# Decays computed beside the triangular inverse in a bidirectional RWKV-7 / GLA trunk, with root, share and block-deal settings changed

## The chip, the cores and the metric

One core of one Trainium2 chip runs the whole program. The metric is the device time of one execution in microseconds (us); the kernel before has a median of 1413.8 us over three runs (1413.56 to 1420.72).

The engines are named as in the profile: PE (TensorE matmuls; PEld its weight loads), DVE (VectorE), ACT (ScalarE), POOL (GpSimd), SP (SyncE, which issues most DMAs). A name such as L806 is a line of the kernel before.

## The reference, cut to what matters

Two layers of a trunk run on 640 tokens (128 of a prompt, 512 of a sample), width 1024. Layer 0 has a short gated convolution and a bidirectional RWKV-7 mixer with 16 heads of 64; layer 1 is chunked gated linear attention. The change touches layer 0 alone, and in it these quantities of the RWKV-7 mixer, for two directions:

```
w_raw = w0 + tanh(h @ w1) @ w2
decay = exp(-exp(-softplus(-w_raw) - 0.5))
iclr  = sigmoid(a0 + (h @ a1) @ a2)
kk    = k * k_k;  kk = kk / max(sqrt(sum(kk * kk)), 1e-12)
k_mod = k * (1 + (iclr - 1) * k_a)
s     = s * w_t - (s @ kk_t) (kk_t * a_t) + v_t k_t        (token by token)
gn    = (o - mean(o)) * rsqrt(var(o) + 64e-5)
bonus = sum(r * (k_mod of both directions) * r_k) * v
```

`iclr` is called the rate below. The kernel does the recurrence in chunks of 64 tokens: a chunk needs the running products of the decays, a masked 64 by 64 matrix G, and the inverse of a unit triangular part of it.

## The kernel before, in words

**Order.** Matrix instructions on PE run in the order in which the program writes them. Instructions of the other engines are placed by a scheduler at compile time: each engine takes the ready instruction of the best priority, so work can be pulled ahead of where it is written, until a tile that it needs is still held by an earlier user. Each tile name (tag) has a fixed number of buffers.

**Periods.** The 16 heads are taken as 8 pairs. After a prologue (head pair 0) come periods 0 to 7; period hp runs the state chain of pair hp, in 8 steps (`chain_step`, L957) of 6 gaps each, and prepares pair n = hp + 1 in these 48 gaps. Each gap also gets a share of the dense matmuls: blocks of 48 matmuls of 320 columns (`dense`), which project the input for v, k, r, z of the pairs and for the convolution tiles. `Period` (from L1151) deals the blocks' cost (a planner's 134 ns a matmul) to the gaps in proportion to `base` plus the planner's costs of the small work due in the gap; `share` multiplies the weights of some gaps (the prologue's gaps 5 to 9 by `psh`). `CN` and `NC0` say how many of the 32 convolution blocks go to which place. In a paired gap (all periods but the prologue) small work stands before the dense matmuls of an even gap and behind those of an odd gap.

**Small work of a period** (`period`, L1275; lists of gaps in `PR`):
- `expand_all` (L809), eight units at the gaps of `ex`: the first two are `expand` (L747) for direction 0, chunks 0 to 4 and 5 to 9; the other six are `pairs` (L792), PE's matmuls for G of 4, 4 and 2 chunks in each direction, their masked evictions on DVE (L806), and, with the first two, `expand` for direction 1. `expand` makes Pq and iP (exp of the decays' running sums, ACT L757 and L758), the operands `ar` and `bk` on DVE (L765 to L790). Pq and iP have one buffer each, and Pq shares it with `X_i`, the state at the start of the chain (L923).
- `inv_a` (L871) at the gap `inv`: G's triangular 32 by 32 blocks go to DRAM and back as 80 lanes (`Ai`), are inverted there by 30 pairs of dependent DVE instructions (L880, L882), and go back by DRAM into G. `Ai` is a tile of the tag `lw`, which also holds the decays.
- `inv_b` (L894) at `ib`: DVE transposes (L902) and PE's `pT` matmuls complete the inverse.
- `bonus` (L854) at `bo`: adds the two directions' modified rates (L857), multiplies by r (L858), then the sums on PE.
- `p_lr` (L448) for the pair after, at `lr`, when `bonus` is done: for the rates (tags `ta0`, `ta1`) and then the decays (`lw`), four times two PE matmuls (`plr_ta`, `plr_lw`) and an ACT tanh (L478); for the decays also two ACT scalings (L482) and four DVE scans (L487). Its weights come by two DMAs (L453), an ACT rounding (L455) and a POOL difference (L461).
- `p_kk` and `p_kb` (L709, L735): norms of kk; `fin_s`, `fin_b`, `fin_t` (L1054 to L1110): group norm and gate of the pair before; `chain_init`, `vrows`.

`p_kk` and `fin_s` call `rsqrt` (L207), a bit trick and three Newton rounds: 11 DVE instructions on 10 columns. Other norms of the kernel use POOL's power instruction (L286, L1622).

**Around the periods.** The prologue has 32 unpaired gaps. Period 6 loads six stored convolution tiles back (`load_conv`, L1197), two of them into `lw`; period 7 starts the output projection and uses `ta0`, `ta1` and `lw` for parts of a later modulation (`gemv`, L1257). Layer 1 follows and is not touched.

Of the kernel before, what the change touches and what calls it, by code (L numbers as in the profile page):

```python
# [127 lines left out]
def tile_trunk(ctx, tc, A, O):  # L128
# [319 lines left out]
    def p_lr(hp):  # L448
# [16 lines left out]
        lw, ta = [], []
        for (lst, i, boff, tg) in ((ta, 1, 16, "ta"), (lw, 0, 0, "lw")):
            if not i:
                low(0, raw0)
                lwt = el.tile([P, 2, TOK], F32, tag="lw", name=f"lw{hp}")
            for d in range(2):  # L470
                o = et(f"{tg}{d}", f"{tg}{hp}_{d}") if i else lwt[:, d]
                b = der[:, boff + d * 8 + hp:boff + d * 8 + hp + 1]
                for s in range(2):
                    ps = pm(f"plr{hp}_{d}_{tg}_{s}")
                    t = slice(s * HT, (s + 1) * HT)
                    mm(ps[:, 0:HT], w2h[i][:, d], hlr[i, d][:, t], start=True, stop=False)
                    mm(ps[:, 0:HT], w2l[i][:, d], hlr[i, d][:, t], start=False, stop=True)
                    evict(lambda: S.activation(o[:, t], ps[:, 0:HT], AF.Tanh, scale=0.5, bias=b))  # L478
                    yield 270
                lst.append(o)  # L480
# [1428 lines left out]
```

## Time and profile before

| what | value |
|---|---|
| median of three runs | 1413.8 us |
| the profiled execution | 1424.3 us, of which the span is 1422.5 us |
| mean granted TensorE clock | 0.949 of full speed |
| PE busy | 1307.4 us (92%) |
| DVE busy | 960.6 us (68%) |
| ACT, POOL busy | 739.0 us (52%), 461.8 us (32%) |

The profiled execution is one run, 10.5 us longer than the median. PE's busy time counts matmuls at whatever clock was granted; the granted clock has two levels, 1.2 and 2.4 GHz, which the profile shows as 0.5 and 1.0. A row of the timeline gives the start and the length in us, the engine, the line, the operation, the tiles written and read, the shapes, the count of merged instructions, and in brackets the idle time before it with what ended it.

The prologue's dense part runs from about 55 us to 189 us of the span, periods 0 to 7 from there to about 1020 us.

### The profile page before, as it was taken

The page shows a single profiled execution, that of the slowest core. Times are in us where ns is not written, and L with a number is a line of the kernel's source. Part 1 is how long each engine was busy: PE and PEld are TensorE (multiplying, and loading weights), DVE is VectorE, ACT ScalarE, POOL GpSimd, SP SyncE. Part 2 cuts the span into 40 slices and gives each one's busy share as a digit, 9 for nine tenths or more (in the row PEclk, how much of TensorE's full clock was granted, in tenths as well). Part 3 has the DMA queues.
Part 4 walks back from the last instruction along what each step waited for, and adds up shares of the span by engine and source line. Part 5 has one row for each costly group of instructions (what it writes and reads, how often), then busy time and mean ns, then how long its engine had stood idle before and what let it go on. Part 6 is the DMA issues. An engine that isn't in the chain of part 4 may idle for free.

```text
span 1422.5 us, 32431 instructions
## 1 busy us (share of the span) xinstructions
PE 1307.4 (92%) x12279; PEld 1193.4 (84%) x12279; DVE 960.6 (68%) x2218; ACT 739.0 (52%) x2054; POOL 461.8 (32%) x596
## 2 busy tenths in 40 slices
PE   8889899998998988989989989789989999999997
PEld 3779888987887977978978968779889889999997
DVE  5375646977776885786686778675966596646454
ACT  3553264575565565555746655544445764434341
POOL 1433332222222222222322213334466343343232
PEclk9988998999999999989989999788999999999998
DMA  9112222212212212212212232455644322322143
GB/s 355 59 57 79 66 66 57 63 61 67 64 59 61 68 44 70 66 46 71 68 44 60 69 80 65 122 176 162 185 126 137 99 70 79 98 86 85 53 130 105
DMA packets 139629, 127.15 MB, mean 89 GB/s; under 512 B 54096, under 2 KB 121936, under 8 KB 139472
## 3 DMA queue, kind: packets, MB, share of 16 engines
q1 hardware_dynamic: 136912, 118.38, 28.0%
q0 software_dynamic: 2016, 6.16, 1.1%
q8 instruction: 97, 1.59, 0.5%
q14 instruction: 60, 0.49, 0.1%
q10 hardware_dynamic: 544, 0.52, 0.1%
HBM read 108.37 MB, written 16.65 MB: 88 GB/s over the span
## 4 chain that ended last, share of the span: by engine, by line
PE 45%; DVE 26%; ACT 4%; DMA 4%; issue 4%; POOL 1%; SPq 0%; POOLq 0%; DVEq 0%; ACTq 0%
PE pd_zg L135 4%; PE pd_oo L135 4%; PE pd_zw L135 3%; PE pd_qk L135 3%; PE pd_k L135 3%; DVE Ai L882 3%; PE pu L135 3%; PE pd_zc L135 3%; DVE Ai L880 2%; PE pd_eoc L135 2%; PE pd_gc L135 2%; PE pa L135 2%; DVE gacc L247 2%; PE pd_vg L135 2%; DVE bk L790 2%
## 5 line engine op out<-in xcount | busy, mean ns | idle before, releaser
L880 DVE TENSOR_TENSOR Ai<-Ai 80x30 f32<-80x30 f32 (+14 forms) x240 | 95.1, 396 | 36.9 <-DMA Ai<-Ad 30.0
L882 DVE TENSOR_TENSOR Ai<-Ai 80x30 f32<-80x30 f32 (+14 forms) x240 | 96.8, 403 | 6.8
L135 PE MATMUL pG<-ar,bk 64*128 64x128 f32 x640 | 69.5, 325 | 30.8 <-DVE bk L790 18.4
L135 PEld LDWEIGHTS pG<-ar,bk 64*128 64x128 f32 x640 | 54.0, 215 | 45.3 <-DVE bk L790 18.4
L806 DVE TENSOR_TENSOR G<-pG,con 128x512 f32<-128x512 f32 (+1 forms) x96 | 53.2, 595 | 23.5 <-PE pG L135 23.1
L247 DVE SCALAR_TENSOR_TENSOR gacc<-gw,cf,gacc 128x512 f32<-128x512 f32 x70 | 60.2, 891 | 10.1 <-DMA gw<-in_ada_dram 9.8
L1022 ACT ACTIVATE VU<-pa 64x192 f32<-64x192 f32 (+1 forms) x128 | 38.3, 299 | 55.0 <-PE pa L135 53.8
L333 POOL TENSOR_TENSOR lo_eoc<-wr_eoc,hi_eoc 128x256 fp32r<-128x256 f32 x48 | 44.9, 946 | 45.7 <-ACT hi_eoc L330 35.1
L1037 DVE SCALAR_TENSOR_TENSOR X<-pu,PC,XP 128x64 f32<-128x64 f32 x144 | 33.1, 274 | 27.4 <-PE pu L135 24.8
L333 POOL TENSOR_TENSOR lo_gc<-wr_gc,hi_gc 128x256 fp32r<-128x256 f32 x32 | 27.8, 876 | 70.9 <-ACT hi_gc L330 70.1
L333 POOL TENSOR_TENSOR lo_gb<-wr_gb,hi_gb 128x256 fp32r<-128x256 f32 x32 | 25.4, 800 | 73.5 <-ACT hi_gb L330 44.4
L135 PE MATMUL pd_gc<-hi,hi_gc 128*128 128x320 f32 x128 | 43.4, 339 | 4.5 <-ACT cy L446 2.1
L333 POOL TENSOR_TENSOR lo_zw<-wr_zw,hi_zw 128x256 fp32r<-128x256 f32 x32 | 27.2, 861 | 62.7 <-ACT hi_zw L330 56.3
L135 PE MATMUL pd_eoc<-hi,lo_eoc 128*128 128x320 f32 x128 | 44.0, 343 | 3.2 <-POOL lo_eoc L333 3.2
L991 ACT ACTIVATE XP<-X,PC 128x64 f32<-128x64 f32 x120 | 35.8, 342 | 21.1 <-DVE X L1037 20.8
L135 PE MATMUL pd_zc<-hi,hi_zc 128*128 128x320 f32 x128 | 42.7, 334 | 4.3 <-DVE cv L683 2.5
L333 POOL TENSOR_TENSOR lo_r<-wr_r,hi_r 128x256 fp32r<-128x256 f32 x32 | 25.0, 787 | 65.5 <-ACT hi_r L330 51.5
L333 POOL TENSOR_TENSOR lo_zc<-wr_zc,hi_zc 128x256 fp32r<-128x256 f32 x32 | 24.8, 781 | 65.3 <-ACT hi_zc L330 60.6
L333 POOL TENSOR_TENSOR lo_u<-wr_u,hi_u 128x256 fp32r<-128x256 f32 x32 | 26.8, 840 | 59.2 <-ACT hi_u L330 56.8
L135 PE MATMUL pd_k<-hi,hi_k 128*128 128x320 f32 x112 | 37.3, 333 | 9.4 <-ACT k L446 3.8
L135 PE MATMUL pd_eoc<-hi,hi_eoc 128*128 128x320 f32 x128 | 44.9, 351 | 0.9 <-ACT hi_eoc L330 0.9
L333 POOL TENSOR_TENSOR lo_k<-wr_k,hi_k 128x256 fp32r<-128x256 f32 x28 | 23.5, 841 | 65.1 <-ACT hi_k L330 63.8
(482 smaller groups left out, 5075.9 us busy)
## 6 DMA issues: line engine op xcount, KB each, us to landing
gw<-in_ada_dram SPq DMA_DIRECT2D x64, 256.0 KB, 3.2
gw<-in_ada_dram SPq DMA_DIRECT2D x16, 512.0 KB, 7.9
wr_eoc<-in_eo_dram SPq DMA_DIRECT2D x48, 128.0 KB, 2.7
wr_qk<-in_ow_dram SPq DMA_DIRECT2D x33, 128.0 KB, 2.3
wr_r<-in_ew_dram SPq DMA_DIRECT2D x32, 128.0 KB, 2.4
wr_v<-in_ew_dram SPq DMA_DIRECT2D x32, 128.0 KB, 2.5
wr_u<-in_ew_dram SPq DMA_DIRECT2D x32, 128.0 KB, 2.3
wr_gc<-in_ew_dram SPq DMA_DIRECT2D x32, 128.0 KB, 2.3
```

The lines of the kernel that those rows point to most:

```text
L135: tc.keep_in_program_order(T.matmul(*a, **kw))
L247: V.scalar_tensor_tensor(acc[j], w, c, acc[j], op0=ALU.mult, op1=ALU.add)
L333: le.tensor_tensor(lo, w, hi.bitcast(F32), op=ALU.subtract)
L790: E(2).tensor_tensor(bk[HS[h], :, h], ta3[HS[h]], iP3[HS[h]], op=ALU.mult)
L806: V.tensor_tensor(g, x, mk, op=ALU.mult)
L880: V.tensor_tensor(tt, Ai[:, 0:i, i:i + 1].to_broadcast([80, i, n]), Ai[:, i:i + 1, i + 1:].to_broadcast([80, i, n]), op=ALU.mult)
L882: V.tensor_tensor(Ai[:, 0:i, i + 1:], Ai[:, 0:i, i + 1:], tt, op=ALU.add)
L991: S.activation(XP[:, l], X[:, l], AF.Copy, scale=PC[:, s, l:l + 1])
L1022: S.activation(VU[HB[h], h, 0:nl], pr[HB[h], 0:nl], AF.Copy, scale=-1.0)
L1037: V.scalar_tensor_tensor(Xn[:, l], po[:, 0, l], PC[:, s, l:l + 1], XP[:, l], op0=ALU.mult, op1=ALU.add)
```

## The change

- `p_lr` is split in two parts with generators of their own: the decays (part 0) at gaps 17 to 21 (`lrw`) as soon as the pair's G is made, and the rates (part 1) at gaps 43 to 47 as soon as the inverse is written. Each part loads its own weights. The rates of both directions are now one tile of the tag `ta`.
- `Ai` takes the tag `ta` in place of `lw`. The two DVE instructions at the head of `bonus` become `bonus_a`, due just before `inv_a`.
- `ex` goes from gaps 0, 1, 5, 7, 9, 11, 12, 13 to 0, 1, 4, 5, 6, 8, 9, 10; `inv` from 14 to 11; `fb`, `ft` from 14 and 17 to 20, to 12 and 13 to 16. Period 0 keeps its `ex0` and `inv0`; its rates' and decays' order is exchanged.
- `rsqrt` becomes one POOL power instruction, for its 16 calls.
- `psh` goes from 0.1 to 1.0, `pib` (the prologue's `inv_b`) from gaps 28 to 31 to gaps 30 to 31. One convolution block more in the prologue (`NC0` 8), one less in period 1; period 6 takes its convolution blocks ahead of z.
- `load_conv` puts tiles 4 and 5 into `ta`; `gemv` uses `ta` as one tile.

The diff, cut:

```
-PR = {'NC0': 7,
- 'CN': [[2, 1, 1], [2, 1, 1], [1, 1, 1], [1, 1, 1], [1, 1, 1], [1, 1, 1], [2, 1, 1]],
+PR = {'NC0': 8,
+ 'CN': [[2, 1, 1], [1, 1, 1], [1, 1, 1], [1, 1, 1], [1, 1, 1], [1, 1, 1], [2, 2, 2]],
+ 'lrw': [17, 21],
- 'pib': [28, 31],
+ 'pib': [30, 31],
- 'psh': 0.1,
+ 'psh': 1.0,
- 'ex': [0, 1, 5, 7, 9, 11, 12, 13],
- 'inv': 14,
+ 'ex': [0, 1, 4, 5, 6, 8, 9, 10],
+ 'inv': 11,
- 'lr': [39, 47],
+ 'lr': [43, 47],
- 'fb': 14,
- 'ft': [17, 20],
+ 'fb': 12,
+ 'ft': [13, 16],
...
     def rsqrt(x, n):
-        y, t = (cst.tile([P, 20], F32, tag=g, name=f"{g}{next(ids)}")[:, 0:n] for g in ("rsy", "rst"))
...
+        G.tensor_tensor(x, x, mhalf[:, 0:n], op=ALU.pow)
...
-    def p_lr(hp):
+    def p_lr(hp, part):
...
-        low(1, load(1))
-        raw0 = load(0)
+        low(part, load(part))
         yield 0
...
+        boff, tg = ((0, "lw"), (16, "ta"))[part]
+        x = el.tile([P, 2, TOK], F32, tag=tg, name=f"{tg}{hp}")
...
+        for d in range(2 if not part else 0):
+            S.activation(x[:, d], x[:, d], AF.Identity, scale=-0.5 * CW, bias=mcw)
...
+    def bonus_a(hp):
+        q = st[hp]
+        ta, r = q["ta"], q["r"]
+        E(7).tensor_tensor(ta[0], ta[0], ta[1], op=ALU.add)
+        E(8).tensor_tensor(r, ta[0], r, op=ALU.mult)
+        yield 0
...
-        At = el.tile([80, 2 * TOK], F32, tag="lw", name=f"Ai{hp}")
+        At = el.tile([80, 2 * TOK], F32, tag="ta", name=f"Ai{hp}")
...
-                misc += [Work(PRE, p_lr(n + 1), 9, *PR["lr" if hp else "lr0"], 270, (n, "b")), ...
+                misc += [Work(PRE, p_lr(n + 1, 0), 5, *PR["lrw"], 270, (n, "g")), Work(PRE, p_lr(n + 1, 1), 5, *PR["lr"], 270, (n, "i")), ...
```

The last argument of a `Work` is what it needs: "g" is G made, "i" the inverse written, "b" the bonus done. The settings of period 6 (`ex6`, `inv6`, `fb6`, `ft6`) change as `ex`, `inv`, `fb`, `ft` do.

## Rows read from the trace of the kernel before

**Rows 1.** The page: TensorE's granted clock in 40 slices of the span

```profile
PEclk9988998999999999989989999788999999999998
```

**Rows 2.** Windows: stretch, us, busy us (instructions) by engine, PE's clock, DMA

```profile
93.40:113.90 20.50, 14.93 (x74) 12.19 (x75) 16.32 (x32) 6.23 (x19) 0.97 (x2) 0.50 0.11 24
133.10:154.20 21.10, 21.10 (x146) 21.10 (x146) 19.90 (x44) 5.80 (x14) 8.71 (x11) 1.00 0.27 86
...
738.50:748.80 10.30, 9.46 (x53) 8.17 (x54) 5.44 (x11) 2.01 (x5) 1.46 (x2) 0.50 0.10 28
892.10:902.40 10.30, 7.74 (x110) 7.16 (x112) 2.99 (x6) 3.48 (x8) 1.46 (x2) 0.50 0.37 77
919.40:926.30 6.90, 5.43 (x39) 5.35 (x40) 6.90 (x13) 3.83 (x11) 3.14 (x3) 0.51 0.54 175
```

**Rows 3.** Windows of the prologue; the last one of tile cv alone (DVE, ACT, POOL)

```profile
89.90:119.90 30.00, 23.44 (x139) 19.71 (x138) 20.41 (x37) 12.31 (x34) 6.25 (x9) 0.66 0.15 39
119.90:165.50 45.60, 43.84 (x291) 42.52 (x289) 36.44 (x83) 12.03 (x30) 19.50 (x24) 1.00 0.28 82
165.50:188.90 23.40, 19.28 (x257) 18.90 (x257) 6.52 (x21) 9.28 (x22) 6.71 (x10) 0.85 0.32 87
...
113.00:131.00 18.00, 4.06 (x8) 0.81 (x1) 0.00 (x0) 0.98 0.31 87
```

**Rows 4.** PE's waits by releaser: total us, times, longest

```profile
PE pG L135 <- DVE bk L790: 18.4, 18, 1.8
PE pG L135 <- DVE G L806: 11.6, 6, 4.4
PE pT L135 <- DVE oac L902: 8.4, 4, 4.0
PE pa L135 <- DVE X L1037: 7.8, 7, 2.6
PE pa L138 <- ACT VU L1022: 4.4, 3, 1.8
```

**Rows 5.** Timeline of PE: the prologue's longest waits

```profile
97.32 2.07 PE L135 MATMUL pG<-ar,bk 64*128 64x128 f32 x14 [4.40 <-DVE G L806]
...
169.18 0.28 PE L135 MATMUL pT<-oac,G 32*32 32x32 f32 x2 [3.67 <-DVE oac L902]
```

**Rows 6.** Timelines of DVE, ACT and PE: the head of period 3

```profile
505.64 1.67 DVE L487 TENSOR_TENSOR_SCAN lw<-con,lw 128x320 f32<-128x320 f32 x2 [2.36 <-ACT lw L482]
...
506.88 0.47 ACT L757 ACTIVATE Pq<-lw 128x320 f32<-128x320 f32 x1 [0.35 <-PE pu L135]
...
515.05 1.16 PE L135 MATMUL pG<-ar,bk 64*128 64x128 f32 x14 [1.76 <-DVE bk L790]
```

**Rows 7.** The expansion of period 3: its window, and a row of PE's timeline

```profile
507.30:534.00 26.70, 22.32 (x222) 19.86 (x223) 26.03 (x64) 14.68 (x47) 6.16 (x8) 0.87 0.15 38
...
529.53 0.41 PE L135 MATMUL pd_zc<-hi,hi_zc 128*128 128x320 f32 x1 [2.53 <-DVE cv L683]
```

**Rows 8.** POOL's powers on one tile; the Newton roots' DVE time in two windows

```profile
L286 POOL TENSOR_TENSOR rs<-rs,mhalf x5: 707/862/1177, 15.5 to 1414.2; 128x3 f32<-128x3 f32 x2, 128x2 f32<-128x2 f32 x2, 128x5 f32<-128x5 f32 x1
...
0.00:1422.50 1422.50, 35.27 (x128) 0.95 0.30 89
...
0.00:1422.50 1422.50, 12.76 (x48) 0.95 0.30 89
```

**Rows 9.** Timelines of PE, DVE and POOL: periods 6 and 7

```profile
894.36 0.31 PE L135 MATMUL pT<-oac,G 32*32 32x32 f32 x2 [4.00 <-DVE oac L902]
...
912.99 1.49 DVE L214 SCALAR_TENSOR_TENSOR rst<-rst,gst 128x10 f32<-128x10 f32 x1
...
912.89 1.56 POOL L1212 TENSOR_TENSOR lo<-oraw,hi 128x640 fp32r<-128x640 f32 x1
...
920.87 0.90 PE L135 MATMUL pa<-X,ar 64*64 64x64 f32 x12 [2.56 <-DVE X L1037]
...
1047.69 0.95 PE L138 MATMUL pgn<-con,oac 128*128 128x128 f32 x5 [3.60 <-DVE oac L1085]
```

More of the change, by code (lines that the diff above doesn't have):

```diff
@@ L72 @@
  'sh': 0.25,
- 'ex6': [0, 1, 5, 7, 9, 11, 12, 13],
- 'inv6': 14,
+ 'ex6': [0, 1, 4, 5, 6, 8, 9, 10],
+ 'inv6': 11,
  'vr6': 26,
@@ L77 @@
  'init6': 43,
- 'fb6': 14,
- 'ft6': [17, 20],
+ 'fb6': 12,
+ 'ft6': [13, 16],
  'kb6': [2, 3],
@@ L461, in low @@
             G.tensor_tensor(w2l[i], w2, w2h[i].bitcast(F32), op=ALU.subtract)
-        low(1, load(1))
-        raw0 = load(0)
+        low(part, load(part))
         yield 0
[L465 to L480, printed above, removed]
@@ L481, in p_lr @@
-        for d in range(2):
-            S.activation(lw[d], lw[d], AF.Identity, scale=-0.5 * CW, bias=mcw)
+        boff, tg = ((0, "lw"), (16, "ta"))[part]
+        x = el.tile([P, 2, TOK], F32, tag=tg, name=f"{tg}{hp}")
+        for d in range(2):
+            b = der[:, boff + d * 8 + hp:boff + d * 8 + hp + 1]
+            for s in range(2):
+                ps = pm(f"plr{hp}_{d}_{tg}_{s}")
+                t = slice(s * HT, (s + 1) * HT)
+                mm(ps[:, 0:HT], w2h[part][:, d], hlr[part, d][:, t], start=True, stop=False)
+                mm(ps[:, 0:HT], w2l[part][:, d], hlr[part, d][:, t], start=False, stop=True)
+                evict(lambda: S.activation(x[:, d, t], ps[:, 0:HT], AF.Tanh, scale=0.5, bias=b))
+                yield 270
@@ L491, in tile_trunk @@
+        st[hp][tg] = [x[:, d] for d in range(2)]
     new_h()
@@ L594, in tile_trunk @@
                 ahead["r0", q] = weights(A["ew"][32], "r0", q)
-            lr0 = p_lr(0)
+            lr0 = (x for part in (1, 0) for x in p_lr(0, part))
             next(lr0)
@@ L1198, in load_conv @@
         for k, t in zip(ks, tags):
-            if k > 1:
+            if k in (0, 4):
+                x = el.tile([P, 2, TOK], F32, tag=t, name=f"oraw{k}")
+                raws[k], raws[k + 1] = x[:, 0], x[:, 1]
+            elif k not in (1, 5):
                 raws[k] = et(t, f"oraw{k}")
-            elif k == 0:
-                x = el.tile([P, 2, TOK], F32, tag="lw", name="oraw01")
-                raws[0], raws[1] = x[:, 0], x[:, 1]
             nc.sync.dma_start(raws[k], oT[k * P:(k + 1) * P])
@@ L1257, in gemv @@
     def gemv(b):
-        if b % 2:
-            a2 = el.tile([P, 2, TOK], F32, tag="lw", name=f"gacc{b}")
-            acc = [a2[:, j, 0:512] for j in range(2)]
-        else:
-            acc = [el.tile([P, 512], F32, tag=t, name=f"gacc{b}_{t}") for t in ("ta0", "ta1")]
+        a2 = el.tile([P, 2, TOK], F32, tag=("ta", "lw")[b % 2], name=f"gacc{b}")
+        acc = [a2[:, j, 0:512] for j in range(2)]
         stage = ("r", "kk") if b < 6 else ("r", "kk", "sz")
@@ L1286, in period @@
             if hp == 0 and PR["lr1"]:
-                misc += [Work(PRE, p_lr(1), 9, *PR["lr1"], 270)]
+                misc += [Work(PRE, (x for part in (0, 1) for x in p_lr(1, part)), 10, *PR["lr1"], 270)]
             misc += [Work(PRE, expand_all(n), 8, PR["ex" + z] if hp else PR["ex0"], None, 540, (n, "r"))]
@@ L1290, in period @@
             iv = iv if hp else PR["inv0"]
-            misc += [Work(EV + 500, inv_a(n), 1, iv, iv, 0, (n, "g")), Work(PRE, inv_b(n), 2, *PR["ib" if 0 < hp < 6 else "ib0"], 1000, (n, "i")), Work(CH, chain_init(n), 1, ci, ci, 0), Work(PRE, vrows(n), 1, vr, vr, 850, (n, "v")), Work(PRE, bonus(n), 2, *PR["bo" + z], 540, (n, "w"))]
+            misc += [Work(PRE, bonus_a(n), 1, iv, iv, 0, (n, "g")), Work(EV + 500, inv_a(n), 1, iv, iv, 0, (n, "g")), Work(PRE, inv_b(n), 2, *PR["ib" if 0 < hp < 6 else "ib0"], 1000, (n, "i")), Work(CH, chain_init(n), 1, ci, ci, 0), Work(PRE, vrows(n), 1, vr, vr, 850, (n, "v")), Work(PRE, bonus(n), 2, *PR["bo" + z], 540, (n, "w"))]
             a, b, c = PR["CN"][hp]
@@ L1317, in tile_trunk @@
     prio(PRE)
[L1318 removed]
+    w1 = []
     r0 = p_r(0)
```

27 lines of the change are left out of this document (8 added, 19 removed).

## The prediction

> **What bounds the kernel now.** I read the page's clock line first, then PE's waits, then windows of the stages, then timelines where a wait was long. PE is busy for 1307.4 of 1422.5 us, so only PE's holes and its slow stretches can be won back: 115 us idle, and the slices where the clock line shows less than 9 [rows 1]. At full clock 146 matmuls fill 21.1 us, 0.145 us each, 6.9 us for a block of 48 [rows 2]. Stretches that follow waits run at 0.5, the lower of the two levels; work there takes twice as long, so such a stretch costs up to half its length [rows 2].
>
> Three places matter. The prologue's G matmuls take 30.0 us for 139 matmul records at a mean clock of 0.66 [rows 3]; 80 of them are pG (1.16 us for 14 [rows 6], so 6.6 us), the rest at most 59 × 0.145 = 8.6. So 15 of the 30 us are a hole: `psh` keeps the dense work out of it. DVE is busy 20.41 us there [rows 3], and PE waits 4.40 us for one of its evictions [rows 5]. Second, in the periods PE waits most for the operands bk (18.4 us) and the evictions of G (11.6 us) [rows 4]. Third, single waits at the ends of periods 6 and 7 (4.00, 2.56 and 3.60 us [rows 9]).
>
> **The change, part by part.** The profiled execution is 1424.3 us; the sum is a difference against it, and I apply it to the median, 1413.8 us, which is 0.7% lower.
>
> *Prologue, even share and one block more.* The planner's weights (750 a gap plus due work) come to 29,185 before, with the tenth, and 35,530 after; 12 and 13 blocks of 6,452 are dealt. Times 0.145/0.134, a unit of weight is 2.87 ns before and 2.55 ns after. Gaps 0 to 5 then hold 22.5 us of dense work instead of 20.5: PE comes to the first pairs 2.0 us later. Gaps 6 to 10 hold 18.7 instead of 7.6 us, 11 us more. Together 13 us, which fit into the 15 us hole if DVE keeps up. It gets the first convolution's gc, gb and zc evictions and sums in this stretch, twelve instructions; eight of them take 4.06 us [rows 3], so some 6.1 (an estimate): 26.5 of 30 us, just enough. So the last pairs stay near 119.9 us, and with them the inverse. Dense work from there to `inv_b` is 40.5 us (gaps 11 to 29) instead of 41.2 (gaps 11 to 27); PE meets the same wait for the inverse (3.67 us [rows 5]). Behind it 8.95 instead of 14.4 us are left: the prologue ends 5.4 us earlier, and period 1 loses a block, 6.9 us. That is −12.3; for holes that stay I take **−9 us**. The ends: −15 (the whole hole) and 0 (all of it comes back as a wait for the inverse).
>
> *Decays at gaps 17 to 21.* Moved are 8 matmuls (1.2 us, the same count elsewhere in PE's order), 4 tanh, 2 scalings, 4 scans (1.67 us for two [rows 6]), one weight DMA on SP with its ACT rounding and POOL difference. The scans now stand beside the inverse on DVE, at lower priority, and lengthen it by at most 3.3 us; it starts three gaps earlier, so nothing waits. Does the expansion start sooner? **No**: its first Pq waits for PE's pu, the last reader of X_i, which owns Pq's buffer, and starts at 506.88, before the second pair of scans is through [rows 6]. What the head of a period gains is ACT time, where the chain's VU copies made PE wait 4.4 us in all [rows 4]. I take **−4**, bounds −4.4 and 0.
>
> *`ex` and `inv` earlier.* PE reaches the first pairs two gaps, 2.4 us, earlier: 510.4 instead of 512.8 in period 3 (the wait before 515.05 [rows 6], less 0.46 of two matmuls). From there to the fifth pairs it has 13.4 us of work: 3.7 sets of pairs of 1.3, three pairs of gaps of 2.0 to 2.4, and some 1.7 of the chain's matmuls (0.90 us for 12 at half clock [rows 9]). So it needs the fourth expansion at 524. DVE was busy 26.03 of the 26.70 us from Pq to that point, 534 [rows 7]: it is the bound here. Of these 26 us the roots (2.5), late parts of the group norm (0.8) and the bonus pair (1.6) fall away or come later: 529 to 530. PE then waits some 6 us; before it waited 1.76 at the first pairs [rows 6] and 2.53 for an eviction behind them [rows 7], 4.3 in all, each with a stretch at half clock behind it. I take **+2 us for periods 1 to 5 together**, bounds −8 and +30 (the slower rival).
>
> *`bonus_a`* keeps its two instructions; the `ta` buffer is free before G's last block is in DRAM, so nothing new waits. *Period 0* keeps its gaps: 0.
>
> *Roots.* The 16 Newton roots are 176 instructions, 35.27 + 12.76 = 48.0 us of DVE, 3.0 us each [rows 8]. POOL's power takes 707, 862 and 1177 ns on 2, 3 and 5 columns [rows 8], 157 ns a column: an estimate of 2.0 us on 10; between 1.2 (the 5-column row) and 2.0 I take 2.0. POOL is at 32%. What a POOL instruction does to DVE is in the trace: a root's step that takes 0.17 us elsewhere took 1.49 us beside a POOL subtraction of 1.56 us [rows 9]. The Trainium skill, "SBUF — State Buffer", Who interferes with whom, says that a DVE instruction with two SBUF inputs and a GpSimd instruction that reads SBUF exclude each other for the whole instruction. By that rule each power may hold DVE for up to 2.0 us; the row above agrees, no row shows a power beside such an instruction. Without a hold DVE gains 3.0 us a root, with one 1.0; I count neither beyond the sum above, and period 7.
>
> *Period 6.* Its inverse returns too late: PE waits 4.00 us [rows 9] and 10.3 us at half clock follow [rows 2]. Three gaps earlier (2 us each there) covers the wait. **−6**, bounds −9 and −3. *Period 7.* The roots among other work delay the chain's X (2.56 us) and then the pgn transposes (3.60 us) [rows 9], with 6.9 us at half clock [rows 2]. **−6**, bounds −9 and 0 (the power queued behind POOL's subtractions).
>
> Sum: −9 − 4 + 2 − 6 − 6 = **−23**; 1413.8 − 23 = **1391 us** (in the profiled execution about 1401). Its own range, from the bounds of prologue, period 6 and 7, is 1378 to 1403.
>
> **The rivals.**
> 1. *Half of it*: DVE cannot carry the convolution's evictions in the prologue's hole; the pairs end 6 us later, PE waits that much longer for the inverse, and of −12.3 about −5 stays; periods 6 and 7 give half. −5 − 2 + 3 − 6 = −10: 1404 us (1397 to 1411). For it: 26.5 of 30 us on DVE is an estimate.
> 2. *No change*: the denser expansion eats what the rest gives, +3 us in each of periods 1 to 6: 1391 + 18 = 1409 us. It is also the case in which "beside the inverse" buys nothing, since the head of the period waits for X_i.
> 3. *Slower*: DVE is the bound from gap 4 to gap 10 of periods 1 to 6. If the powers hold it 2 us at the period's head and nothing falls away, the fourth expansion comes at 534 as now, PE waits 10 us where it now waits 4.3, and a stretch like 738.5 to 748.8 at half clock [rows 2] costs 5 us. Some +6 us in each of six periods, +36, less 9 + 4 + 6 of the gains above, from 1413.8: 1431 us. It turns the sign from about +4 us a period on, that is when the fourth expansion of period 3 would end later than about 532. For it: 97% DVE [rows 7]. Against: 3 us of roots and scans leave this stretch.
>
> **How the numbers follow.** Chances: forecast 0.45, rival 1 0.20, rival 2 0.12, rival 3 0.23. About 0.5% (7 us) is what a measurement here can tell from no change, so faster is below 1407, slower above 1421. Faster: 0.45 and three quarters of rival 1, 0.60. Slower: 0.23. Same: 0.17. The range runs from the forecast's lower bound to the near half of rival 3, 1376 to 1425; it leaves out about 0.05 below and 0.13 above.
>
> **What would show it.** Right: in the prologue no stretch of 20 us at 0.5 and a chain that starts near 184 us; no pT wait in period 6; no pgn wait at the end of period 7. PE's first pairs some 2 us earlier in periods 2 to 5, waits for bk and G there of the same sum as now. Wrong: those two groups well above 30 us with the clock at 0.5 behind them (rival 3), a pT wait in the prologue above 8 us (rival 1), or powers that start long after their input on POOL.

## The result, and the profile after

The changed kernel takes 1436.2 us (median of 4 executions, 1432.4 to 1439.8), the kernel before 1417.3 us in the same comparison. The measured ratio is 1.0101, with a 95% interval of 1.0065 to 1.0138 (the two medians, of four executions each, give 1.0134): about 1% slower, where 1391 us was forecast. The profiled execution of after took 1432.4 us (span 1430.5), that of before 1424.3 (1422.5).

The page of the kernel after, engines and granted clock [rows 1], then its windows of the prologue [rows 3]:

```profile
PE 1305.5 (91%) x12279; PEld 1192.3 (83%) x12279; DVE 942.2 (66%) x2042; ACT 734.6 (51%) x2054; POOL 504.5 (35%) x612
...
PEclk9899999999999999999999999989989999999998
...
89.90:119.90 30.00, 25.98 (x195) 23.62 (x194) 25.70 (x45) 12.06 (x34) 10.76 (x12) 0.94 0.22 61
165.50:188.90 23.40, 17.99 (x239) 17.30 (x238) 6.28 (x18) 7.86 (x20) 6.82 (x8) 0.78 0.29 69
```

PE's waits by releaser in the kernel after [rows 4]: total us, times, longest.

```profile
PE pa L136 <- DVE X L1028: 28.4, 23, 2.7
PE pG L136 <- DVE bk L776: 19.7, 15, 1.7
PE pG L136 <- DVE G L792: 8.7, 7, 3.3
PE pT L136 <- DVE oac L893: 7.2, 5, 4.8
PE pa L139 <- ACT VU L1013: 2.0, 5, 0.5
```

The prologue's hole is filled (195 matmul records instead of 139, clock 0.94 instead of 0.66), VU and G cost less, bk hardly more. One line has grown: X, the chain's state, from 7.8 us in 7 waits to 28.4 in 23. DVE is less busy than before (942 against 961 us), yet PE stands more often for it.

By periods, from one pair's first XP on ACT to the next pair's: periods 1 to 5 last 512.8 us before (293.9 to 806.7) and 524.2 after (296.5 to 820.7), although period 1 lost a block of 6.9 us, so 18.3 us are to be found. PE's idle time there grew from 40.8 to 56.0 us, 15.2 more, and the time at half clock from 34.0 to 40.9 us, which costs half of that, 3.4: 18.6 together. The half-clock part belongs to these two executions: the mean granted clock of the kernel before goes from 0.949 to 0.971 over its executions on record. Of the idle time X makes 21.0 us instead of 2.0. Period 6 went from 96.9 to 94.5 us, and what follows from 518.8 to 515.3.

One of these waits, in period 3, by DVE's and PE's timelines of the kernel after:

```profile
567.06 0.38 DVE L871 TENSOR_TENSOR Ai<-Ai 80x210 f32<-80x210 f32 x1
567.47 0.37 DVE L873 TENSOR_TENSOR Ai<-Ai 80x210 f32<-80x210 f32 x1
567.76 0.81 DVE L473 TENSOR_TENSOR_SCAN lw<-con,lw 128x320 f32<-128x320 f32 x1
568.50 0.36 DVE L871 TENSOR_TENSOR Ai<-Ai 80x220 f32<-80x220 f32 x1
568.78 0.81 DVE L473 TENSOR_TENSOR_SCAN lw<-con,lw 128x320 f32<-128x320 f32 x1
569.51 0.36 DVE L873 TENSOR_TENSOR Ai<-Ai 80x220 f32<-80x220 f32 x1
569.79 0.47 DVE L1028 SCALAR_TENSOR_TENSOR X<-pu,PC,XP 128x64 f32<-128x64 f32 x2
...
565.63 0.40 PE L136 MATMUL pu<-VU,G 128*64 128x64 f32 x8
...
570.21 0.45 PE L136 MATMUL pa<-X,ar 64*64 64x64 f32 x8 [2.22 <-DVE X L1028]
```

PE has finished pu, all that X needs, at 566.0. DVE gets to X at 569.8: between them stand steps of the inverse (Ai) and two scans of the decays. X has the best priority of all, but the scheduler fixed the order at compile time, and on the chip X does not pass what is ahead of it. (That the scheduler expected pu later, or DVE earlier, than the chip had them is inferred; no run shows its times.) The Trainium skill, "PSUM — Partial Sum Buffer", Engine vs sequencer instructions, says that VectorE's queue is a strict FIFO; these rows agree: DVE is busy without a break from 567.1 us on, and X comes after all that was queued ahead of it.

Waits of this kind come at step 4 of each of periods 1 to 5, at step 6 behind the tail of the inverse, and at step 7 behind a root (0.2 us of PE's time in most periods, 2.1 in period 3):

```profile
597.37 1.99 POOL L207 TENSOR_TENSOR rn<-rn,mhalf 128x10 f32<-128x10 f32 x1 [0.64 <-DVE rn L713]
...
599.40 1.01 DVE L716 COPY rnb<-rn 128x640 f32<-128x640 f32 x1 [2.10 <-POOL rn L207]
...
514.88 0.42 ACT L447 ACTIVATE w2h<-w 128x256 fp32r<-128x256 f32 x1 [3.36 <-DMA w<-in_w_dram]
515.21 0.46 ACT L743 ACTIVATE Pq<-lw 128x320 f32<-128x320 f32 x1
...
905.90 0.24 PE L136 MATMUL pT<-oac,G 32*32 32x32 f32 x2 [1.29 <-DVE oac L893]
```

The first two rows are a power root and DVE standing 2.10 us for it, with X queued behind. The next two show ACT standing 3.36 us for the rates' late weights with Pq behind them: Pq of period 3 starts 5.4 us behind that period's first pa for X_i (509.8), before it was 3.9. The last is period 6's wait for the inverse, 1.29 instead of 4.00 us [rows 9]; the pgn wait of 3.60 us at period 7's end is gone.

Nor did the inverse come back earlier. In period 3 it starts 50.1 us into the period instead of 54.7 and ends 83.6 us into it instead of 84.0: it takes 33.6 us (556.2 to 589.7) where it took 29.3. Over periods 2 to 5 two things have grown between its first and last step: DVE's other work, by 3.2 us on average, as much as the four scans take, and the inverse's own 60 instructions, from 23.3 to 25.5 us in sum. Some nine tenths of what these take beyond the shortest time of their shape lie in steps that overlap a POOL instruction.

### The profile page after: what moved, and what is told of

It reads as the page before. It is cut to its first block, busy times and chain, and to the rows that moved or that the text cites. A ratio compares the mean times of both kernels' runs of the same rounds, so it can differ in the third digit from the quotient of the medians.

```text
span 1430.5 us, 32264 instructions
## 1 busy us (share of the span) xinstructions
PE 1305.5 (91%) x12279; PEld 1192.3 (83%) x12279; DVE 942.2 (66%) x2042; ACT 734.6 (51%) x2054; POOL 504.5 (35%) x612
## 4 chain that ended last, share of the span: by engine, by line
PE 44%; DVE 33%; DMA 8%; issue 5%; ACT 5%; POOL 4%; SPq 0%; DVEq 0%; POOLq 0%; ACTq 0%
DVE Ai L871 6%; DVE Ai L873 6%; DMA gw<-in_ada_dram 4%; PE pd_oo L136 4%; PE pd_zg L136 3%; PE pd_qk L136 3%; PE pd_zw L136 3%; PE pd_k L136 2%; PE pd_vg L136 2%; DVE gacc L239 2%; PE pa L136 2%; PE pd_gb L136 2%; PE pG L136 2%; PE pd_zc L136 2%; PE pd_u L136 2%
## 5 line engine op out<-in xcount | busy, mean ns | idle before, releaser
L871 DVE TENSOR_TENSOR Ai<-Ai 80x30 f32<-80x30 f32 (+14 forms) x240 | 104.3, 435 | 14.8 <-DMA Ai<-Ad 8.5
L239 DVE SCALAR_TENSOR_TENSOR gacc<-gw,cf,gacc 128x512 f32<-128x512 f32 x112 | 96.8, 909 | 18.8 <-DMA gw<-in_ada_dram 18.6
L873 DVE TENSOR_TENSOR Ai<-Ai 80x30 f32<-80x30 f32 (+14 forms) x240 | 98.1, 409 | 6.3
L136 PE MATMUL pG<-ar,bk 64*128 64x128 f32 x640 | 66.0, 314 | 29.3 <-DVE bk L776 19.7
L792 DVE TENSOR_TENSOR G<-pG,con 128x512 f32<-128x512 f32 (+1 forms) x96 | 53.1, 593 | 13.3 <-PE pG L136 13.1
L1028 DVE SCALAR_TENSOR_TENSOR X<-pu,PC,XP 128x64 f32<-128x64 f32 x144 | 33.1, 274 | 42.9 <-PE pu L136 42.6
L325 POOL TENSOR_TENSOR lo_eoc<-wr_eoc,hi_eoc 128x256 fp32r<-128x256 f32 x48 | 44.4, 937 | 40.2 <-ACT hi_eoc L322 30.9
L982 ACT ACTIVATE XP<-X,PC 128x64 f32<-128x64 f32 x120 | 35.8, 342 | 39.2 <-DVE X L1028 38.8
L136 PEld LDWEIGHTS pa<-X,ar 64*64 64x64 f32 x512 | 20.9, 136 | 41.4 <-issue 39.6
L136 PE MATMUL pa<-X,ar 64*64 64x64 f32 x512 | 28.0, 234 | 28.6 <-DVE X L1028 28.4
L325 POOL TENSOR_TENSOR lo_zc<-wr_zc,hi_zc 128x256 fp32r<-128x256 f32 x32 | 28.6, 901 | 65.2 <-ACT hi_zc L322 37.7
L325 POOL TENSOR_TENSOR lo_v<-wr_v,hi_v 128x256 fp32r<-128x256 f32 x32 | 23.6, 742 | 74.6 <-ACT hi_v L322 53.8
L325 POOL TENSOR_TENSOR lo_gb<-wr_gb,hi_gb 128x256 fp32r<-128x256 f32 x32 | 27.1, 852 | 64.8 <-ACT hi_gb L322 34.4
L325 POOL TENSOR_TENSOR lo_r<-wr_r,hi_r 128x256 fp32r<-128x256 f32 x32 | 28.3, 892 | 52.6 <-ACT hi_r L322 50.6
L325 POOL TENSOR_TENSOR lo_gc<-wr_gc,hi_gc 128x256 fp32r<-128x256 f32 x32 | 26.6, 836 | 56.5 <-ACT hi_gc L322 29.9
L136 PE MATMUL pd_v<-hi,lo_v 128*128 128x320 f32 x128 | 44.8, 350 | 0.0
```

What stands on the lines that cost most here:

```text
L136: tc.keep_in_program_order(T.matmul(*a, **kw))
L239: V.scalar_tensor_tensor(acc[j], w, c, acc[j], op0=ALU.mult, op1=ALU.add)
L325: le.tensor_tensor(lo, w, hi.bitcast(F32), op=ALU.subtract)
L792: V.tensor_tensor(g, x, mk, op=ALU.mult)
L871: V.tensor_tensor(tt, Ai[:, 0:i, i:i + 1].to_broadcast([80, i, n]), Ai[:, i:i + 1, i + 1:].to_broadcast([80, i, n]), op=ALU.mult)
L873: V.tensor_tensor(Ai[:, 0:i, i + 1:], Ai[:, 0:i, i + 1:], tt, op=ALU.add)
```

## The experiments

Ratios are against the kernel before on the same chip, with a 95% interval. X is PE's wait for X in the profiled execution, over the whole run; "inverse" is the mean time from the first to the last Ai instruction of periods 2 to 5.

| kernel | ratio | X, us | bk, us | inverse, us |
|---|---|---|---|---|
| before | 1 | 7.8 | 18.4 | 30.1 |
| after | 1.0101 [1.0065, 1.0138] | 28.4 | 19.7 | 35.6 |
| prologue_alone | 0.9965 [0.9940, 0.9990] | 8.7 | 19.0 | 29.8 |
| roots_alone | 0.9986 [0.9967, 1.0006] | 11.0 | 18.2 | 29.8 |
| split_alone | 1.0071 [1.0044, 1.0098] | 22.9 | 14.1 | 36.7 |
| gaps_alone | 1.0088 [1.0061, 1.0115] | 17.6 | 24.9 | 32.8 |
| split_scans_late | 1.0077 [1.0050, 1.0104] | 24.9 | 14.0 | 36.6 |
| after_scans_late | 1.0103 [1.0077, 1.0129] | 30.7 | 20.0 | 35.8 |
| split_decays_23 | 1.0073 [1.0048, 1.0098] | 20.2 | 13.5 | 37.3 |
| split_decays_36 | 0.9980 [0.9959, 1.0002] | 10.9 | 12.8 | 33.9 |
| split_scans_behind | 1.0029 [1.0010, 1.0048] | 16.8 | 15.1 | 34.0 |
| expansion_gaps_alone | 1.0040 [1.0016, 1.0064] | 7.1 | 25.4 | 30.9 |
| finish_gaps_alone | 0.9970 [0.9949, 0.9990] | 12.0 | 18.5 | 29.9 |
| after_decays_36 | 1.0075 [1.0050, 1.0100] | 23.7 | 18.9 | 33.1 |
| after_decays_36_old_finish | 0.9980 [0.9960, 1.0000] | 9.5 | 19.7 | 32.1 |
| after_36_gn_on_pool | 1.0043 [1.0020, 1.0065] | 18.8 | 19.8 | 31.8 |
| prologue_roots_p6 | 0.9943 [0.9920, 0.9967] | 8.7 | 19.7 | 30.2 |
| parts_kept_with_split | 1.0022 [1.0000, 1.0044] | 15.2 | 16.7 | 30.3 |
| parts_kept_no_split | 0.9971 [0.9952, 0.9989] | 8.2 | 22.7 | 29.9 |
| kept_with_late_decays | 1.0022 [0.9997, 1.0046] | 9.5 | 15.8 | 34.0 |

All kernels at 1.007 or more have X at 17 us or more; none with X at 12 us or less is above 1.004. The bk column has no such order. Part of X lies outside the periods that the change slows: in period 7 it is 4.0 us before, 4.6 after, and up to 7.7 in other runs. In periods 1 to 5 alone PE waits for X 2.0 us before, 21.0 after, 13.1 in split_alone, 10.3 in gaps_alone, 2.5 in split_decays_36, 5.6 in split_scans_behind, 15.8 in after_decays_36 and 0.6 in after_decays_36_old_finish.

**The four parts, each alone.** The kernel before takes one part of the diff at a time.

```
split_alone     p_lr(hp, part), bonus_a, 'lrw': [17, 21], 'lr': [43, 47], Ai on the tag "ta"
roots_alone     rsqrt: G.tensor_tensor(x, x, mhalf[:, 0:n], op=ALU.pow)
prologue_alone  'psh': 1.0, 'NC0': 8, 'pib': [30, 31], CN[1] = [1, 1, 1], CN[6] = [2, 2, 2]
gaps_alone      ex, inv, fb, ft and ex6, inv6, fb6, ft6 as after
```

> The kernel before with the split of decays and rates alone: the decays with their four scans at gaps 17 to 21, the inverse's buffer on the rates' tag, the conv tags that follow from it. Newton roots, the old gaps of the expansion and the old prologue stay. Theory 1 (the scans, 0.81 us each, stand ahead of the chain's X in DVE's queue): two of them in front of X cost about 2 us of PE wait and some 1 to 2 us of half clock in each of periods 1 to 5, less what the head of the period gains: ratio to the kernel before 1.005 to 1.012, and in the trace PE's waits for X at 15 us or more (7.8 before). Rival A (the denser expansion is the loss): the split alone is neutral or better, ratio 0.995 to 1.002, X near 8 us. Rival C (the later load of the rates' weights at the period's end holds ACT at the head of the next): ratio near 1.003 and a wait of over 3 us of ACT for w at each head, as in the kernel after.

> The kernel before with the power roots alone. Theory 1: 48 us of DVE's Newton work go, POOL takes 2.0 us a root in their place; the wait for pgn at the end of period 7 goes or shrinks (3.6 us and some half clock), the rest is neutral: ratio 0.995 to 1.000. Rival B (powers hold up DVE, or DVE stands for them with X queued behind): ratio 1.003 to 1.008, with waits of DVE for rn of 1 to 2 us in most periods and X late behind them.

> The kernel before with the even first part and the new deal alone (psh 1.0, NC0 8, the inverse's return at 30 to 31, one convolution block less in period 1). As my prediction costed it: -9 us, ratio 0.994; the end of the prologue stays near 206 us with a block more in it and period 1 is about 7 us shorter. Rival D (the settings cost what they gain): ratio 0.999 to 1.003.

> The kernel before with the earlier gaps of expansion, inverse, finish b and the transposes alone, in all periods (the decays and rates stay together at gaps 39 to 47, Newton roots). Theory 1 (the loss of the change is scans and powers ahead of X): the gaps alone cost little, ratio 0.998 to 1.004, PE's waits for bk and G together below 36 us (30 before). Rival A (the denser expansion is the loss): ratio 1.008 to 1.02, with the waits for bk and G at 36 us or more and a first half clock stretch behind the first pairs in each of periods 1 to 5.

The product of the four ratios is 1.0110; the change measured 1.0101. With intervals of a quarter of a percent on each ratio the two agree; that the parts add is not shown by it, and runs further down have parts that do not. Two parts gain 0.5% together (the roots' share is within their interval), two lose 0.7 and 0.9%. Rival A and theory 1 had each put the loss into one part, and it lies in both. The split has X at 22.9 us, as theory 1 asked; the gaps cost more than it allowed, with bk and X both up. Rival B falls: with powers alone DVE stands for rn too, but X rises only to 11.0 us and the time does not.

**What in the split costs.** First the scaling and the scans alone were to move behind the inverse (a new `p_scan`; `p_lr` with False leaves them out), in the split and in the kernel after:

```
-Work(PRE, p_lr(n + 1, 0), 5, *PR["lrw"], 270, (n, "g"))
+Work(PRE, p_lr(n + 1, 0, False), 5, *PR["lrw"], 270, (n, "g")),
+Work(PRE, p_scan(n + 1), 2, 41, 42, 0, (n, "i"))
```

> The split alone once more (1.0071 of the kernel before), but the scaling and the four scans of the decays go to gaps 41 and 42 of each period, behind the inverse; weights, matmuls and tanh stay at gaps 17 to 21. Theory 1 (the split loses by the scans' 3.3 us among the inverse, which puts X behind more inverse steps): the loss goes, ratio 0.997 to 1.002, PE's waits for X fall from 22.9 us to about 8 to 10, and the inverse of periods 2 to 5 is back from 35 to 37.5 us to about 30. Rival C (where the weights' load and the rates' tanh stand is the loss): ratio stays at 1.005 to 1.009 with X near 8 us.

> The kernel after with the scaling and the scans of the decays at gaps 41 and 42 instead of beside the inverse, all else as in the change. Theory 1: the part of the split (0.7%) comes back and the part of the gaps (0.9%) stays: ratio to the kernel before 1.002 to 1.005 (after: 1.0101), PE's waits for X from 28.4 to about 18 us. If the denser gaps alone put X behind the inverse, as their run has it (17.6 us of X), X cannot fall below that.

Nothing changed, but the runs don't speak against theory 1. DVE's timeline of split_scans_late, period 1:

```profile
352.60 0.81 DVE L488 TENSOR_TENSOR_SCAN lw<-con,lw 128x320 f32<-128x320 f32 x1
353.33 0.36 DVE L886 TENSOR_TENSOR Ai<-Ai 80x220 f32<-80x220 f32 x1
353.61 0.81 DVE L488 TENSOR_TENSOR_SCAN lw<-con,lw 128x320 f32<-128x320 f32 x1
354.34 0.84 DVE L888 TENSOR_TENSOR Ai<-Ai 80x220 f32<-80x220 f32 x1
355.11 0.46 DVE L1043 SCALAR_TENSOR_TENSOR X<-pu,PC,XP 128x64 f32<-128x64 f32 x2
```

The scans still stand among the inverse, right ahead of X. A gap sets where an instruction is written; the scheduler pulled the scans forward as soon as the tanh were done. Both runs are repeats of split and after, and inconclusive; within these two pairs X differs by 2.0 and 2.3 us, a measure of how far one profiled execution can be off. The trace of split_alone gave another suspect meanwhile: DVE stands 2.8 to 3.6 us for ACT's gn among the inverse, where the tanh stand between ACT's evictions. So the whole decays were moved, a little and far, in the split alone: `'lrw': [23, 27]` and `'lrw': [36, 40]`.

> The split alone with the decays at gaps 23 to 27 instead of 17 to 21: still beside the inverse, but behind the gaps in which ACT evicts the group norm's transposes (17 to 20). Theory 2 (in the split alone the four tanh and two scalings of the decays stand on ACT between the evictions of gn, and DVE, with the inverse queued behind its gn sum, stands 2.8 to 3.6 us for them): that wait falls below 1 us, the inverse of periods 2 to 5 shortens from 35 to 37.5 us to about 33, PE's waits for X fall from 22.9 to below 15 us, ratio 0.999 to 1.004. Theory 1 (the scans' own 3.3 us beside the inverse): gn is gone but X stays near 20 us, ratio 1.005 to 1.008.

> The split alone with the decays at gaps 36 to 40, where the inverse is over or in its last steps. Both theories: gn's wait below 1 us, the inverse back at 29 to 32 us, X at 8 to 12 us, ratio 0.997 to 1.002. If it stays at 1.005 or more, the loss of the split is neither scans nor tanh beside the inverse, but what the moved buffers and the later rates do at the head of a period.

PE's waits for X in split_decays_23, split_decays_36 and split_scans_behind (below):

```profile
PE pa L136 <- DVE X L1037: 20.2, 13, 2.8
```

```profile
PE pa L136 <- DVE X L1037: 10.9, 11, 2.5
```

```profile
PE pa L136 <- DVE X L1040: 16.8, 14, 2.6
```

Beside the inverse at gap 23 the loss stays; behind it at gap 36 it is gone. Theory 2 falls as well: with the decays at 36, DVE still stands 3.4 to 4.1 us for gn in periods 2 to 5, no less than at 23 (3.6 to 4.1), and nothing is lost. What differs is DVE's other work between the inverse's first and last step: 8.1 to 12.3 us in periods 2 to 5 with the decays at 23, 4.8 to 8.0 at 36, 3.2 to 4.3 us less, of which four scans of 0.81 us are 3.2. Rival C is not the main loss either: with the decays at 36 ACT still stands 1.7 to 2.8 us for weights at the heads of periods 1 to 5, where in split_alone it stands 1.8 to 3.5. A last run held the scans behind the inverse by data: at the end of `inv_a` one instruction makes the scaling's bias from the inverse's diagonal, which is 1:

```
+V.tensor_tensor(mcb[0:80], af[:, 0:1], mcw[0:80], op=ALU.mult)
-S.activation(x[:, d], x[:, d], AF.Identity, scale=-0.5 * CW, bias=mcw)
+S.activation(x[:, d], x[:, d], AF.Identity, scale=-0.5 * CW, bias=mcb)
```

> The split alone (decays at gaps 17 to 21, 1.0071, X 22.9 us) with a data dependence that holds the scaling and the four scans of the decays behind the inverse: the scaling's bias is a copy that one DVE instruction writes from the inverse's unit diagonal when the inverse is through. Weights, matmuls and tanh stay at gaps 17 to 21. (split_scans_late was to do this by its gaps, but the scans there still ran among the inverse.) Theory 1 (the scans' 3.3 us among the inverse are the loss): the inverse of periods 2 to 5 falls from 35 to 37.5 us to 32 to 35, other DVE work in it by 3 us or more, X from 22.9 to about 11 us, ratio 0.996 to 1.002, as with the decays at 36 (0.9980). If the matmuls and tanh beside the inverse are the loss: X stays above 18 us, ratio 1.005 to 1.008.

This time they are behind it (split_scans_behind, DVE, period 3):

```profile
581.89 0.21 DVE L884 TENSOR_TENSOR Ai<-Ai 80x30 f32<-80x30 f32 x1
582.96 2.97 DVE L484 TENSOR_TENSOR_SCAN lw<-con,lw 128x320 f32<-128x320 f32 x4 [0.87 <-ACT lw L479]
```

The inverse falls to 34.0 us and PE's wait for X in periods 1 to 5 from 13.1 to 5.6 us. The ratio falls from 1.0071 to 1.0029, neither theory's number: by these two the scans are more than half of the split's loss, though the two intervals together allow anything from a tenth of a percent to all of it. Matmuls and tanh at gaps 17 to 21 are still there; that they, or their shift of the order, keep the rest, against 0.9980 with all of it at 36, was not tested.

**What in the gaps costs.** The gaps were divided in the kernel before: expansion and inverse alone (`ex`, `inv`, `ex6`, `inv6`), finish alone (`fb`, `ft`, `fb6`, `ft6`). And in the kernel after, the decays alone were moved to 36, with the new finish and with the old one of periods 1 to 5:

```
after_decays_36               'lrw': [36, 40]
after_decays_36_old_finish    'lrw': [36, 40], 'fb': 14, 'ft': [17, 20]
```

> The kernel before with the earlier gaps of the expansion and of the inverse alone (ex, inv, ex6, inv6); finish b and its transposes stay at gaps 14 and 17 to 20. The gaps together gave 1.0088. If the density of the expansion is the loss (bk later at the first pairs, the inverse among other work): ratio 1.006 to 1.010, bk near 24 us and X near 17 us again. If it is finish b and its transposes, which at gaps 12 to 16 push DVE work against the start of the inverse: ratio 0.998 to 1.003, X near 10 us.

> The kernel before with the earlier gaps of finish b and of its transposes alone (12 and 13 to 16); expansion and inverse keep theirs. By the difference of the two runs on gaps (1.0088 together, 1.0040 for expansion and inverse) the rest is 0.5%: ratio 1.003 to 1.007, with X behind the inverse and DVE standing for gn. If instead the finish only hurts together with the earlier inverse, which it then meets: ratio 0.998 to 1.002, X near 8 us.

> The kernel after with the decays alone moved from gaps 17 to 21 to gaps 36 to 40; the earlier finish, expansion and inverse stay. If the decays beside the inverse are the one part that matters (0.9 to 1.0% between gaps 23 and 36 in the split alone): ratio 0.999 to 1.003, X near 10 us. If the finish among the start of an earlier inverse costs as well (1.0088 for all gaps, 0.9970 and 1.0040 for the two halves of them): ratio 1.004 to 1.008, X at 15 to 18 us.

> The kernel after with two of its settings taken back: the decays at gaps 36 to 40 instead of 17 to 21, finish b and its transposes at 14 and 17 to 20 in periods 1 to 5. Theory 2: what made X late behind the inverse goes (gn's wait and the ACT work ahead of it), X falls from 28.4 to 8 to 14 us; the bk waits of the denser expansion stay near 20 us. Sum of the parts: -0.35% prologue, -0.15% roots, +0.4% expansion, 0 for the split: ratio 0.997 to 1.002. If X stays above 20 us, theory 2 is wrong.

The denser expansion costs 0.4%, with bk at 25.4 us. The earlier finish alone gains 0.3%, against the expectation. Together they cost 0.9%: they interact, and the same shows in the kernel after, where two gaps of the finish make 1.0075 out of 0.9980, with X from 9.5 to 23.7 us. The start of the inverse of period 4 on DVE in after_decays_36:

```profile
658.32 0.19 DVE L871 TENSOR_TENSOR Ai<-Ai 80x30 f32<-80x30 f32 x1 [0.76 <-DMA Ai<-Ad]
658.54 0.18 DVE L873 TENSOR_TENSOR Ai<-Ai 80x30 f32<-80x30 f32 x1
660.32 0.83 DVE L1098 TENSOR_TENSOR gn<-gn,v 128x640 f32<-128x640 f32 x1 [1.60 <-ACT gn L1094]
661.07 0.76 DVE L871 TENSOR_TENSOR Ai<-Ai 80x58 f32<-80x58 f32 x1
661.75 0.81 DVE L1099 TENSOR_TENSOR gn<-gn,sz 128x640 f32<-128x640 f32 x1
...
668.31 0.35 DVE L873 TENSOR_TENSOR Ai<-Ai 80x184 f32<-80x184 f32 x1
668.58 0.47 DVE L1028 SCALAR_TENSOR_TENSOR X<-pu,PC,XP 128x64 f32<-128x64 f32 x2
```

and in after_decays_36_old_finish:

```profile
654.76 0.19 DVE L871 TENSOR_TENSOR Ai<-Ai 80x30 f32<-80x30 f32 x1 [1.93 <-DMA Ai<-Ad]
...
661.85 0.83 DVE L1098 TENSOR_TENSOR gn<-gn,v 128x640 f32<-128x640 f32 x1 [0.88 <-ACT gn L1094]
...
664.41 0.46 DVE L1028 SCALAR_TENSOR_TENSOR X<-pu,PC,XP 128x64 f32<-128x64 f32 x2
```

PE's last matmuls of pu, all that this X needs, in after_decays_36 and then in after_decays_36_old_finish:

```profile
665.42 0.40 PE L136 MATMUL pu<-VU,G 128*64 128x64 f32 x8
```

```profile
663.45 0.40 PE L136 MATMUL pu<-VU,G 128*64 128x64 f32 x8
```

With both earlier, the end of the finish (two instructions on gn and a wait of 1.60 us for ACT) falls on the inverse's first steps and stops it there, and X of step 4 is 2.8 us late. With the old finish it comes 7 us into the inverse and this X makes no wait. But the finish stands ahead of X in both, and X comes about as long after the inverse's first step: 10.3 and 9.7 us here, 10.1 to 10.9 and 9.6 to 11.6 over periods 1 to 5. What differs at step 4 is when pu is done: 7.3 to 8.4 us after the inverse's first step with the new finish, 9.0 to 11.0 with the old one. The inverse's own 60 instructions differ too, 24.8 to 25.8 us in sum with the new finish, 22.9 to 24.0 with the old one; the step at 661.07 above, 0.76 us, takes 0.22 in the other run and overlaps a POOL instruction of 0.94. In finish_gaps_alone gn is through before the inverse starts: none of its instructions stands among the Ai of periods 1 to 5. Is the wait for gn the cause? gn's two instructions went to POOL (`'en': 'VVVGVGVVVVVV'` instead of twelve V):

> after_decays_36 (1.0075, X 23.7 us) with one thing changed: the two sums and products on gn that end the finish (0.81 us each on DVE) go to POOL for pairs 0 to 6. In after_decays_36 DVE stood 1.4 to 1.8 us for ACT's gn some 2 us behind the first step of the inverse, with the inverse and X of step 4 queued behind. If this is how earlier finish and earlier inverse hurt together: no such wait on DVE, X of step 4 no longer late (its 1.1 to 1.4 us go), PE's waits for X from 23.7 to 10 to 16 us, ratio 0.999 to 1.004. If X is late because the inverse's own steps run longer beside POOL or ACT: X stays above 20 us and the ratio at 1.005 or more; POOL's two longer instructions beside the inverse may even add to it.

It came out between the two. The ratio falls to 1.0043 and X to 18.8 us; X of step 6 is no longer late in periods 1 to 5, but PE waits 1.7 to 2.7 us for X of step 4 there, instead of 1.1 to 1.4. DVE's and POOL's timelines of this run say why:

```profile
654.48 0.29 DVE L873 TENSOR_TENSOR Ai<-Ai 80x130 f32<-80x130 f32 x1
654.81 1.56 DVE L871 TENSOR_TENSOR Ai<-Ai 80x150 f32<-80x150 f32 x1
656.41 0.73 DVE L873 TENSOR_TENSOR Ai<-Ai 80x150 f32<-80x150 f32 x1
657.17 1.58 DVE L871 TENSOR_TENSOR Ai<-Ai 80x168 f32<-80x168 f32 x1
...
654.54 1.66 POOL L1098 TENSOR_TENSOR gn<-gn,v 128x640 f32<-128x640 f32 x1 [8.07 <-ACT gn L1094]
656.16 0.80 POOL L325 TENSOR_TENSOR lo_zc<-wr_zc,hi_zc 128x256 fp32r<-128x256 f32 x1
656.92 1.64 POOL L1099 TENSOR_TENSOR gn<-gn,sz 128x640 f32<-128x640 f32 x1
```

An Ai step of 0.31 us (the same 80x150 in period 4 of after_decays_36 takes 0.31) lasts until the POOL instruction beside it ends: the work left DVE and held it none the less. So the wait for gn is at most a part of it. How much the earlier pu, the gn instructions and the steps held by POOL cost each was not separated. That after_decays_36_old_finish came out as theory 2 had it (0.9980, X 9.5 us) is no support for that theory: DVE still stands 0.5 to 2.9 us for gn there.

**What is worth keeping.**

```
prologue_roots_p6      before; prologue and roots as after; ex6, inv6, fb6, ft6 as after
parts_kept_no_split    the same with fb, ft as after
parts_kept_with_split  after; 'lrw': [36, 40]; ex, inv of periods 1 to 5 as before
kept_with_late_decays  the same with fb, ft as before
```

> What the parts alone say is worth keeping: the even first part with its deal, the power roots, and the earlier gaps in period 6 only (there period 6 fell from 96.9 to 91.2 us in the run of the gaps alone); the decays and rates stay together, periods 1 to 5 keep their old gaps. If the parts add, -5 for the prologue, -2 for the roots and -5 for period 6: ratio 0.990 to 0.993. If period 6's gain is given back in period 7, as the later X waits there would have it: 0.994 to 0.996.

> The kernel before with the prologue's settings, the power roots, the earlier finish in all periods and period 6's earlier expansion; decays and rates stay together behind the inverse. If the parts add: 0.9943 of the earlier run times 0.997, ratio 0.989 to 0.993. If period 6's and the finish's gains are the same one: 0.993 to 0.996.

> The kernel after with two settings changed: decays at gaps 36 to 40, and the expansion and the inverse of periods 1 to 5 back at their old gaps (period 6 keeps the new ones, the finish its new ones everywhere). If the parts add (prologue 0.9965, roots 0.9986, split with late decays 0.998, finish 0.997, period 6 about 0.998): ratio 0.987 to 0.992, the best so far. If the earlier rates' buffer and the finish get into each other's way: 0.994 to 0.999.

> The kernel after with decays at gaps 36 to 40 and expansion, inverse and finish of periods 1 to 5 back at their old gaps (period 6 keeps the new ones): what prologue_roots_p6 is (0.9943), plus the split with late decays (0.998 alone). If they add: ratio 0.990 to 0.995, X near 10 us. If the split gives nothing here: 0.995 to 0.999, and prologue_roots_p6 stays the fastest.

prologue_roots_p6 beats both kernels: 1414.2 us against 1421.7, 0.6%. The gain of the finish alone does not come on top, and with the split none of these kernels is faster than before, though the late decays alone were at 0.9980. For kept_with_late_decays X is no explanation (9.5 us); why the split and the even prologue together cost what neither costs alone was not settled. Its trace shows where PE stands instead: 13.7 us for DVE's convolution evictions (cv, cy) in periods 1 to 5, where prologue_roots_p6 has 5.8; no run tests this.

## Why the prediction was wrong

**The step that failed** is that of the decays: the scans "stand beside the inverse on DVE, at lower priority, and lengthen it by at most 3.3 us; it starts three gaps earlier, so nothing waits". The scans' own 3.3 us were right (DVE's other work in the inverse grew by 3.2), but the inverse grew by 5.6, from 30.1 to 35.6 us, with its own steps 2.2 us longer in sum and DVE's wait for gn 1.3 us on average instead of 0.5. "Nothing waits" looked only at who waits for the inverse. The work that stands behind the inverse on DVE is X, the chain itself: priority decides where the scheduler puts an instruction, but once it is queued, a delay of what stands ahead of it can become X's delay, and did: 13.1 us of PE's waits in periods 1 to 5 of split_alone, 2.5 with the decays behind the inverse. −4 was forecast for this part, +0.71%, some 10 us, was measured. Its gain at the period's head is real but smaller: VU 4.4 to 2.0 us, while ACT stands longer for weights (14.3 us in the kernel after, 10.2 before).

**The earlier gaps** were +2 us with bounds −8 and +30; alone they measured +12.2 (1432.8 against 1420.6), inside the bounds. That this lies inside is no support for the sum: the denser expansion, with its bk waits, costs 0.4%, and the rest comes only when the finish moves with it. The sum counted the finish only as DVE time that comes later, and asked of the inverse only when it starts; missed was that the two moves together change where X stands against the inverse on DVE. The expansion fared otherwise, too: PE's first pairs did not come 2 us earlier (13.1 to 13.4 us after the period's first XP in periods 2 to 5, 12.6 to 16.3 before), but the last ones ended 4.8 to 6.7 us earlier, and the wait of some 6 us for the fourth expansion is not in the trace (2.9 us for bk in period 3, both at the first pairs). The bk and G waits were to stay the same in sum: 30.0 before, 28.4 after, right in the kernel after, though not for gaps_alone (34.4).

**Rival 3** gave 1431 us, close to the 1436 measured, by a mechanism that did not happen: bk at 19.7 us is not well above its 18.4, and the powers cost nothing (0.9986 alone). That its number fits is no support for it.

**Prologue**, −9: measured −0.35%, −5 us (interval −8.5 to −1.4). The hole was filled, without a stretch of 20 us at 0.5, and DVE was busy for 25.70 of 30 us against the estimate of 26.5. What failed is that "the last pairs stay near 119.9 us, and with them the inverse". PE's last pairs in the prologue, in the kernel before and in the kernel after:

```profile
119.22 0.71 PE L135 MATMUL pG<-ar,bk 64*128 64x128 f32 x8
```

```profile
124.31 0.72 PE L136 MATMUL pG<-ar,bk 64*128 64x128 f32 x8
```

They end 5.1 us later (5.7 in prologue_alone), the first pT comes at 174.7 us instead of 169.2, and the chain's first pa for X_i at 190.5, where 184 was forecast and 190.8 was before. So the prologue holds a block more but ends no earlier, and the gain is at most that block's 6.9 us in period 1. This is rival 1's account of the prologue, with its −5, although its sign, a pT wait above 8 us there, is missing (the longest is 4.8). What made the pairs late was not tested.

**Roots**: the 2.0 us estimated for a power on 10 columns are 1.98 us in the trace, and counting nothing for them in periods 1 to 6 was about right. **Period 6**, −6: its wait went to 1.29 us, the period only from 96.9 to 94.5. **Period 7**, −6: the pgn wait is gone, as in roots_alone, but PE still waits 2.70 us for X there (3.3 in roots_alone), so the roots were not that wait's cause; all that follows period 6's end gained 3.5 us by the two spans.

The stated ranges do not follow from the bounds given: those of the prologue and of periods 6 and 7 add up to 1379 to 1409 us, not 1378 to 1403. No such end would have held 1436.

## What to carry to other kernels

Before work is put "beside" a long dependent sequence on an in-order engine, list what else is queued there: here the price was paid by the critical instruction that stands behind it, not by the sequence's own consumer. A free share of an engine (DVE 66% busy here) says nothing of this; the waits for that engine by tile do. A move that gains alone can lose together with another when both land on the same stretch (the finish: 0.9970 alone, but 1.0040 becomes 1.0088 with it), so each pair that meets there has to be costed or tried as a pair.
